# Gate and up projections as seven half-block products in fp32, with the down projection after them

## The chip, the cores and the metric

One core of a Trainium2 chip runs the whole kernel in one launch. The metric is the device time of one execution in microseconds (us).

## What is computed

One layer of a streaming encoder: RMS norm, an input projection, two mixers (a state-space group and a chunk-band attention group), an output projection with a residual, and then the feed-forward part. 1024 new frames and 32 frames of a running stream pass through it, 1056 tokens of width 1024. All data are fp32. The part that matters here is the last two lines of `layer`, with `D_FF` = 2816 = 22 blocks of 128:

```python
x = x + jnp.concatenate([y_ssd, o], axis=-1) @ w_out
f = rmsnorm(x, norm_ffn_g)
x = x + (jax.nn.silu(f @ w_gate) * (f @ w_up)) @ w_down
```

## The kernel before

A product of two fp32 matrices is made of three TensorE products: each operand is split into `hi` (rounded to the type fp32r) and `lo` (what is left of it), and hi·hi, hi·lo and lo·hi are summed in PSUM. `split_unit` (L123 to L131) does this for a 512 KB block of weights: SyncE (SP) issues its load into a `raw` buffer, ScalarE (ACT) casts `whi` (L129), and VectorE (DVE) or GpSimd (POOL) subtracts to get `wlo` (L130). The pool `wp` has 3 buffers of `raw` and 5 each of `whi` and `wlo`, shared by all stages. A tiling framework orders the instructions of every engine ahead of time, by the order of the program and by when it reckons that operands and buffers are there, and inserts the semaphores; on the chip every engine then runs its list in that fixed order.

**The tail of the mixer stage** (L842 to L863). Eight tiles of 128 tokens pass through `wout_tile` (second half of the output projection, residual added at L773) and `norm_transpose`: ACT squares and sums (L189), DVE takes the reciprocal root in a dozen short operations (L138 to L146) and scales (`xn`, L192), PE transposes 8 blocks into PSUM (L197), ACT casts `fT_hi` (L200) and DVE subtracts `fT_lo` (L201). `sample_norm` (L802) puts the 32 tokens of the running stream into columns 1024 to 1055. So `fT` and `fL` hold f transposed, 8 blocks of 128 features by 1056 tokens, in hi and lo.

**The feed-forward stage** (L869 to L947). For each of the 22 blocks f of D_FF, `act_block` computes gate and up: `feat_gemm` (L157 to L162) takes 352 tokens at a time (j = 0, 1, 2), 8 blocks of features and 3 products, so 24 matmuls of 352 columns into one PSUM bank. ACT applies SiLU from PSUM (L897), DVE multiplies from PSUM (L895). Then ACT and DVE split the 1024 columns of `act` into `ahi` and `alo` (L910, L911), which stay in SBUF. After every second block, `down` multiplies them with two blocks of `w_down`: for each of 8 token tiles 12 matmuls of 512 columns (`mm3`, L153 to L155), which DVE adds from PSUM to an accumulator `yacc` (L933) that starts out as the residual, loaded once from DRAM. The sample tokens take 8 short matmuls per pair of blocks (L921). The framework mixes the matmuls of `down` with those of the next blocks' gate and up. For the first block, L903 takes j = 0 of gate and up first, which needs the tokens of tiles 0 to 2 alone.

Of the kernel before, what the change touches and what calls it, by code (L numbers as in the profile page):

```python
# [40 lines left out]
def build(tc, a):  # L41
# [142 lines left out]
    def norm_transpose(pl, x, rows, g, dhi, dlo, c0, raw=None, bufs=2, tb="s"):  # L184
# [13 lines left out]
        tv = t.rearrange("p (q c) -> p q c", q=2)[:, :, 0:4 * rows].rearrange("p q (j c) -> p q j c", j=4)  # L198
        h, l = (d[:, :, c0:c0 + rows].rearrange("p (q j) c -> p q j c", q=2) for d in (dhi, dlo))
        nc.scalar.copy(out=h, in_=tv)  # L200
        nc.vector.tensor_tensor(l, tv, h, op=ALU.subtract)  # L201
        if raw is not None:
            nc.vector.tensor_copy(raw.rearrange("p (q j) c -> p q j c", q=2), tv)
# [14 lines left out]
    def norm_tile(t):  # L218
# [6 lines left out]
        steps = norm_transpose(px, x, rows, gmix, hT, hL, t * P, raw=xsT if t == 8 else None)  # L225
        yield from steps
# [572 lines left out]
    fT = hp.tile([P, KB, NT], F32R, tag="hi", name="fT_hi")  # L799
    fL = hp.tile([P, KB, NT], F32R, tag="lo", name="fT_lo")  # L800

    def sample_norm():  # L802
# [22 lines left out]
        for b in range(2):  # L825
            tv = tb[:, b * P:(b + 1) * P].rearrange("p (g q) -> p g q", g=4)
            h = fT[:, b::2, SB:NT]
            nc.scalar.copy(out=h, in_=tv)
            nc.vector.tensor_tensor(fL[:, b::2, SB:NT], tv, h, op=ALU.subtract)
# [36 lines left out]
    yp = pool("yp")  # L869
# [149 lines left out]
```

## Time and profile before

| | us |
|---|---|
| median of 3 runs (1441.91 to 1445.79) | 1445.55 |
| the profiled execution, its own time | 1441.97 |
| its span, first to last instruction | 1440.3 |
| PE busy in the span | 1377.3 (96%) |
| DVE, ACT, POOL busy in the span | 735.5, 387.1, 204.4 |
| mean granted TensorE clock | 0.986 of 2.4 GHz |

Times in the rows are microseconds unless marked ns; L12 is line 12 of the kernel before. PE is the matmul side of TensorE, PEld its weight loads, which overlap the matmuls; DVE is VectorE, ACT ScalarE, POOL GpSimd, SP SyncE with its DMA queue. Matmuls are pipelined, and the profile models their ends, so the duration of one says little; the distance between two starts says what one costs in a stream.

### The profile page before, as it was taken

What the parts mean: (1) busy time and instruction counts of PE and PEld (TensorE: products, weight loads), DVE (VectorE), ACT (ScalarE), POOL (GpSimd) and SP (SyncE); (2) the same over time, 40 slices, a digit from 0 to 9 for tenths busy, and PEclk for the clock granted to TensorE, in tenths of its full rate; (3) what the DMA queues carried; (4) which work ended last, traced back from release to release, by engine and by line L of the source; (5) the groups of instructions that cost most, each with busy time, mean ns of one, the idle gap of its engine ahead of it and who ended that gap; (6) DMA issues with size and microseconds to landing.
All of it is one profiled execution on the core that took longest, in us unless ns stands there. A gap on an engine that the chain in (4) does not pass through costs nothing.

```text
span 1440.3 us, 21840 instructions
## 1 busy us (share of the span) xinstructions
PE 1377.3 (96%) x8864; PEld 1250.0 (87%) x8864; DVE 735.5 (51%) x1506; ACT 387.1 (27%) x711; POOL 204.4 (14%) x193
## 2 busy tenths in 40 slices
PE   5999999779988999999999999999999999999998
PEld 3999998779976778788999999999989898989897
DVE  7446559999987556675232323242423232323323
ACT  6235331323256444434111111111111111112010
POOL 3142255665322101000000000000000000000000
PEclk8999999989999999999999999999999999999999
DMA  6255242447367985756202020202010101010103
GB/s 239 89 189 160 91 155 71 139 142 233 119 212 226 317 264 173 230 162 245 77 15 73 16 73 15 74 23 66 30 59 30 59 30 59 30 59 30 59 1 121
DMA packets 104900, 160.39 MB, mean 111 GB/s; under 512 B 15680, under 2 KB 74112, under 8 KB 104800
## 3 DMA queue, kind: packets, MB, share of 16 engines
q1 hardware_dynamic: 104800, 159.00, 33.7%
q8 instruction: 70, 1.15, 0.3%
q14 instruction: 30, 0.25, 0.1%
HBM read 108.71 MB, written 50.26 MB: 110 GB/s over the span
## 4 chain that ended last, share of the span: by engine, by line
PE 78%; DVE 13%; DMA 5%; issue 2%; ACT 1%; SPq 1%; POOL 0%; DVEq 0%; ACTq 0%; POOLq 0%
PE ps_mm L160 14%; PE ps_mm L162 14%; PE ps_mm L161 13%; PE ps_s L153 6%; PE ps_s L154 6%; PE ps_s L155 6%; PE ps_mm L153 4%; PE ps_mm L154 3%; PE ps_mm L155 3%; PE ps_mm L728 2%; PE ps_t L711 1%; PE ps_t L921 1%; DVE rs_t L145 1%; PE ps_s L689 1%; DVE e L554 1%
## 5 line engine op out<-in xcount | busy, mean ns | idle before, releaser
L160 PE MATMUL ps_mm<-fT_hi,whi 128*128 128x352 f32 x1056 | 341.9, 324 | 0.9 <-DVE x L773 0.9
L162 PE MATMUL ps_mm<-fT_hi,wlo 128*128 128x352 f32 x1056 | 341.3, 323 | 0.0
L161 PE MATMUL ps_mm<-fT_lo,whi 128*128 128x352 f32 x1056 | 339.5, 321 | 0.1
L933 DVE TENSOR_TENSOR yacc<-ps_s,yacc 128x1024 f32<-128x1024 f32 (+1 forms) x89 | 107.8, 1213 | 205.6 <-PE ps_s L155 205.6
L129 ACT CAST whi<-raw 128x1024 fp32r<-128x1024 f32 (+1 forms) x98 | 101.6, 1049 | 388.4 <-PE ps_mm L161 355.7
L160 PEld LDWEIGHTS ps_mm<-fT_hi,whi 128*128 128x128 f32 x1056 | 198.1, 188 | 7.7 <-issue 4.1
L162 PEld LDWEIGHTS ps_mm<-fT_hi,wlo 128*128 128x128 f32 x1056 | 198.8, 188 | 5.3 <-issue 4.1
L161 PEld LDWEIGHTS ps_mm<-fT_lo,whi 128*128 128x128 f32 x1056 | 198.7, 188 | 3.2 <-DVE fT_lo L201 0.4
L153 PE MATMUL ps_mm<-whi,hT_hi 128*128 128x256 f32 (+1 forms) x512 | 150.8, 295 | 3.7 <-ACT hT_hi L200 3.7
L155 PE MATMUL ps_mm<-whi,hT_lo 128*128 128x256 f32 (+1 forms) x512 | 149.8, 293 | 0.8 <-DVE hT_lo L201 0.8
L154 PE MATMUL ps_mm<-wlo,hT_hi 128*128 128x256 f32 (+1 forms) x512 | 149.5, 292 | 0.0
L153 PE MATMUL ps_s<-whi,ahi 128*128 128x512 f32 x352 | 138.7, 394 | 0.0
L154 PE MATMUL ps_s<-wlo,ahi 128*128 128x512 f32 x352 | 137.5, 391 | 0.0
L155 PE MATMUL ps_s<-whi,alo 128*128 128x512 f32 x352 | 135.5, 390 | 0.0
L130 DVE TENSOR_TENSOR wlo<-raw,whi 128x1024 fp32r<-128x1024 f32 x66 | 79.8, 1223 | 100.9 <-ACT whi L129 100.1
L895 DVE TENSOR_TENSOR act<-ps_mm,act 128x352 f32<-128x352 f32 x66 | 34.6, 525 | 180.3 <-PE ps_mm L162 179.8
L153 PEld LDWEIGHTS ps_mm<-whi,hT_hi 128*128 128x128 f32 x512 | 100.7, 197 | 6.4 <-ACT hT_hi L200 4.4
L155 PEld LDWEIGHTS ps_mm<-whi,hT_lo 128*128 128x128 f32 x512 | 100.7, 197 | 1.5 <-DVE hT_lo L201 1.1
L154 PEld LDWEIGHTS ps_mm<-wlo,hT_hi 128*128 128x128 f32 x512 | 100.5, 196 | 0.7 <-issue 0.4
L130 POOL TENSOR_TENSOR wlo<-raw,whi 128x1024 fp32r<-128x1024 f32 (+1 forms) x32 | 77.7, 2435 | 160.6 <-ACT whi L129 159.3
L897 ACT ACTIVATE act<-ps_mm 128x352 f32<-128x352 f32 x66 | 30.5, 462 | 241.4 <-PE ps_mm L162 241.4
L153 PEld LDWEIGHTS ps_s<-whi,ahi 128*128 128x128 f32 x352 | 66.1, 188 | 16.1 <-PE ps_mm L162 4.1
(226 smaller groups left out, 2140.6 us busy)
## 6 DMA issues: line engine op xcount, KB each, us to landing
raw<-in_wgu_dram SPq DMA_DIRECT2D x44, 512.0 KB, 3.4
raw<-in_wd_dram SPq DMA_DIRECT2D x22, 512.0 KB, 4.0
x<-in_xp_dram SPq DMA_DIRECT2D x16, 512.0 KB, 8.1
q<-qst_d SPq DMA_DIRECT2D x32, 256.0 KB, 4.5
mx<-mix_d SPq DMA_DIRECT2D x16, 512.0 KB, 4.5
raw<-in_wq_dram SPq DMA_DIRECT2D x14, 512.0 KB, 4.3
k<-kst_d SPq DMA_DIRECT2D x8, 528.0 KB, 5.5
raw<-in_wx_dram SPq DMA_DIRECT2D x8, 512.0 KB, 4.8
```

Of the source, the lines that this page charges most:

```text
L129: nc.scalar.copy(out=hi, in_=raw)
L130: (eng or nc.gpsimd).tensor_tensor(lo, raw, hi, op=ALU.subtract)
L153: nc.tensor.matmul(ps_, lhsT=lh, rhs=rh, start=start, stop=False)
L154: nc.tensor.matmul(ps_, lhsT=lh, rhs=rl, start=False, stop=False)
L155: nc.tensor.matmul(ps_, lhsT=ll, rhs=rh, start=False, stop=stop)
L160: nc.tensor.matmul(pb[:, 0:G3], lhsT=wh[:, kb, :], rhs=rh[:, kb, c], start=(kb == 0), stop=False)
L161: nc.tensor.matmul(pb[:, 0:G3], lhsT=wh[:, kb, :], rhs=rl[:, kb, c], start=False, stop=False)
L162: nc.tensor.matmul(pb[:, 0:G3], lhsT=wl[:, kb, :], rhs=rh[:, kb, c], start=False, stop=(kb == KB - 1))
L728: nc.tensor.matmul(ob[64 * h:64 * h + 64, 0:nq], lhsT=vs[j][:nkeys[j], 64 * h:64 * h + 64], rhs=rhs, start=(j == 0), stop=(j == nb - 1), t ...
L895: nc.vector.tensor_tensor(act[:, c], pb[:, 0:G3], act[:, c], op=ALU.mult)
L897: nc.scalar.activation(act[:, c], pb[:, 0:G3], AF.Silu)
L933: nc.vector.tensor_tensor(acc_[:, t, w], pb[:, w], acc_[:, t, w], op=ALU.add)
```

## The change

Gate and up are computed by one level of Strassen's algorithm in Winograd's form. Tokens are cut into halves of 528 (512 of the new frames and 16 of the running stream), the 1024 features into halves of 4 blocks of 128, and D_FF into pairs of blocks of 128. Each pair (gate or up, block pair n) is a `quad`: seven products of a 128x512 weight operand with a 512x528 activation operand, in place of eight. A product is 4 blocks of features, 3 terms (hi·hi, hi·lo, lo·hi) and 2 column halves of 264 tokens, so 24 matmuls of 264 columns, into a two-bank PSUM tile of which there are four. There are 22 quads.

- `norm_transpose` ends in a function `put`. In the tail, `put_half` fills `fA` (hi and lo of the first token half, all 8 feature blocks) and `fR` (all of f in plain fp32; ACT copies it from PSUM). `half_sums` makes the sums of quarters in `fR`, in place, on POOL for tiles 4 to 6 and the sample columns and on DVE for tile 7.
- After the tail, five sums are split on whole quarters of 4x528 columns into `T2`, `B22`, `T1`, `T3`, `T4` (ACT casts, DVE subtracts). `sc`, the scratch of the quads, takes the buffer of `fR` (pool `hp`, tag `lo`, one buffer).
- `prep` loads two weight blocks, forms four sums of 512 columns on POOL in place, and makes four split tiles: X (two quarters), V and U (two sums each), W (one quarter). It is called one quad ahead. It draws on the same 5 buffers of `whi` and `wlo`.
- `quad` makes the products in the order A11·B11, S2·T2, A12·B21, S1·T1, S3·T3, S4·B22, A22·T4; ACT copies the first out of PSUM, DVE adds the others from PSUM, seven additions of 528 columns. SiLU and the product of gate and up now read and write SBUF. The finished activations go to DRAM (`act_d`), 4 DMAs per up quad; POOL copies the sample columns.
- The down projection is a loop of its own after the last quad. `act_unit` loads an activation block from `act_d` and splits it; the accumulator is filled by ACT with the first chunk, and the residual is loaded per tile and added by POOL in the second chunk. Its matmuls are those of before.
- The PSUM pool `ps` is closed after the tail, and `pv` takes all 8 banks.

```diff
-    def norm_transpose(pl, x, rows, g, dhi, dlo, c0, raw=None, bufs=2, tb="s"):
+    def norm_transpose(pl, x, rows, g, put, bufs=2, tb="s"):
...
+    fA = hp.tile([P, 2, KB, H], F32R, tag="hi", name="fA")
+    fR = hp.tile([P, KB, 2, H], F32, tag="lo", name="fR")
+    def put_half(kb, half, c, tv):
+        if half == 0:
...
+            nc.scalar.copy(out=hi, in_=tv)
+            nc.vector.tensor_tensor(lo, tv, hi, op=ALU.subtract)
+        r = fR[:, kb, half, c]
+        nc.scalar.copy(out=quads(r) if kb.step is None else r, in_=tv)
+    def half_sums(c, eng):
+        r11, r21, r12, r22 = (fR[:, 4 * k:4 * k + 4, h, c] for h in range(2) for k in range(2))
+        eng.tensor_tensor(r12, r22, r12, op=ALU.subtract)
+        eng.tensor_tensor(r11, r12, r11, op=ALU.add)
+        eng.tensor_tensor(r21, r21, r11, op=ALU.subtract)
...
+        if t >= 4:
+            half_sums(c, nc.vector if t == 7 else nc.gpsimd)
...
+    split_T(T2, r11)
+    split_T(B22, r22)
+    nc.vector.tensor_tensor(r22, r22, r11, op=ALU.subtract)
+    split_T(T1, r22)
+    split_T(T3, r12)
+    split_T(T4, r21)
...
+    sc = hp.tile([P, KB * NT], F32, tag="lo", name="sc")
...
+    def prep(which, n):
+        r1, r2 = (wp.tile([P, 1024], F32, tag="raw", bufs=3, name=nm("raw")) for _ in range(2))
+        for r, f in ((r1, 2 * n), (r2, 2 * n + 1)):
+            nc.sync.dma_start(r, a["wgu"][f, which])
+        a11, a12, a21, a22 = r1[:, 0:512], r1[:, 512:1024], r2[:, 0:512], r2[:, 512:1024]
+        X, V, U, W = ([wp.tile([P, 1024], F32R, tag=tag, bufs=5, name=nm(tag)) for tag in ("whi", "wlo")]
+                      for _ in range(4))
...
+        split(X, r1)
+        split(W, a22)
+        nc.gpsimd.tensor_tensor(a11, a11, a21, op=ALU.subtract)
+        nc.gpsimd.tensor_tensor(a21, a21, a22, op=ALU.add)
+        nc.gpsimd.tensor_tensor(a22, a22, a11, op=ALU.subtract)
+        split(V, r2)
+        nc.gpsimd.tensor_tensor(a12, a12, a22, op=ALU.subtract)
+        split(U, r1)
...
+    def product(A, B):
+        pb = wide()
+        out = in_psum(pb)
+        terms = [(kb, x, y) for kb in range(4) for x, y in ((0, 0), (0, 1), (1, 0))]
+        for n, (kb, x, y) in enumerate(terms):
+            for h in range(2):
+                nc.tensor.matmul(out[:, h, :], lhsT=A[x][:, kb, :], rhs=B[:, y, kb, h * Q:(h + 1) * Q],
+                                 start=(n == 0), stop=(n == len(terms) - 1))
+        return out
+    def quad(ops, dst, use):
...
+        nc.scalar.copy(out=s1, in_=product(ops["A11"], B11))
+        add(u2, s1, product(ops["S2"], T2))
+        add(d[0][0], s1, product(ops["A12"], B21))
+        use(0, 0)
+        add(v, u2, product(ops["S1"], T1))
+        p7 = product(ops["S3"], T3)
+        add(d[1][1], v, p7)
+        use(1, 1)
+        add(u3, u2, p7)
+        add(d[0][1], v, product(ops["S4"], B22))
+        use(0, 1)
+        add(d[1][0], u3, product(ops["A22"], T4))
+        use(1, 0)
...
+            nc.vector.tensor_tensor(o, o, gates[b][h], op=ALU.mult)
+            nc.sync.dma_start(act_d[2 * n + b, :, h, :], o)
+            nc.gpsimd.tensor_copy(asm[:, 2 * n + b, 16 * h:16 * h + 16], o[:, 512:H])
...
+    work = [(w, n) for n in range(NF // 2) for w in range(2)]
+    ops = prep(*work[0])
+    for k, (w, n) in enumerate(work):
+        cur, ops = ops, prep(*work[k + 1]) if k + 1 < len(work) else None
+        quad(cur, acts if w else gates, use_up(n) if w else use_gate)
...
+    def act_unit(f):
+        raw = p5.tile([P, 2, 512], F32, tag="arow", bufs=2, name=nm("arow"))
+        nc.sync.dma_start(raw, act_d[f, :, :, 0:512])
...
+            if first:
+                nc.scalar.copy(out=acc_[:, t, :], in_=pb)
+                continue
+            if c0 == FC:
+                x = p5.tile([P, 1024], F32, tag="res", bufs=2, name=nm("res"))
+                nc.sync.dma_start(x, xb_d[c])
+                nc.gpsimd.tensor_tensor(acc_[:, t, :], x, acc_[:, t, :], op=ALU.add)
...
+    for c0 in range(0, NF, FC):
+        down(c0)
```

## Rows read from the trace of the kernel before

**Rows 1.** The page: busy time of each engine, and the chain that ended last.

```profile
PE 1377.3 (96%) x8864; PEld 1250.0 (87%) x8864; DVE 735.5 (51%) x1506; ACT 387.1 (27%) x711; POOL 204.4 (14%) x193
...
PE 78%; DVE 13%; DMA 5%; issue 2%; ACT 1%; SPq 1%; POOL 0%; DVEq 0%; ACTq 0%; POOLq 0%
```

**Rows 2.** Busy time by stretch: feed-forward stage; columns as in its first line.

```profile
core 0: us, PE busy (x) PEld busy (x) DVE busy (x) ACT busy (x) POOL busy (x), PEclk, DMA share, GB/s
...
700.00:1400.00 700.00, 700.00 (x3987) 642.21 (x3986) 230.05 (x249) 104.40 (x137) 0.00 (x0) 1.00 0.14 44
```

**Rows 3.** Timeline of PE (start, duration): first and last of 166 consecutive 352-column matmuls.

```profile
745.75 0.32 PE L162 MATMUL ps_mm<-fT_hi,wlo 128*128 128x352 f32 x1
...
772.14 0.32 PE L162 MATMUL ps_mm<-fT_hi,wlo 128*128 128x352 f32 x1
```

**Rows 4.** Timeline of PE: first and last of 48 consecutive 512-column matmuls, last down chunk.

```profile
1424.66 0.39 PE L153 MATMUL ps_s<-whi,ahi 128*128 128x512 f32 x1
...
1435.31 0.39 PE L155 MATMUL ps_s<-whi,alo 128*128 128x512 f32 x1
```

**Rows 5.** The page's costliest groups: gate and up (one of three lines), down (one of three).

```profile
L160 PE MATMUL ps_mm<-fT_hi,whi 128*128 128x352 f32 x1056 | 341.9, 324 | 0.9 <-DVE x L773 0.9
...
L153 PE MATMUL ps_s<-whi,ahi 128*128 128x512 f32 x352 | 138.7, 394 | 0.0
```

**Rows 6.** Timeline of PE: first gate matmul, and the transposes of tile 7.

```profile
661.25 0.43 PE L160 MATMUL ps_mm<-fT_hi,whi 128*128 128x352 f32 x1 [0.89 <-DVE x L773]
...
675.56 1.04 PE L197 MATMUL ps_s<-ident,xn 128*128 128x128 f32 x8
```

**Rows 7.** Timeline of PE: first and last of 15 consecutive 264-column matmuls, input projection.

```profile
59.73 0.28 PE L153 MATMUL ps_mm<-whi,hT_hi 128*128 128x264 f32 x1
...
61.44 0.28 PE L155 MATMUL ps_mm<-whi,hT_lo 128*128 128x264 f32 x1
```

**Rows 8.** Groups by line and shape, DVE, ACT and POOL: busy us, mean ns of one, idle before.

```profile
L933 DVE TENSOR_TENSOR yacc<-ps_s,yacc 128x1024 f32<-128x1024 f32 x87 | 106.5, 1225 | 204.1 <-PE ps_s L155 204.1
L130 DVE TENSOR_TENSOR wlo<-raw,whi 128x1024 fp32r<-128x1024 f32 x66 | 79.8, 1223 | 100.9 <-ACT whi L129 100.1
...
L773 DVE TENSOR_TENSOR x<-ps_mm,x 128x512 f32<-128x512 f32 x32 | 22.0, 691 | 28.2 <-PE ps_mm L155 22.2 <-DMA x<-xa_d 3.1 <-DMA x<-in_xp_dram 2.2
...
L145 DVE SCALAR_TENSOR_TENSOR rs_t<-rs_t,rs_m 128x1 f32<-128x1 f32 x78 | 14.9, 192 | 0.9
...
L129 ACT CAST whi<-raw 128x1024 fp32r<-128x1024 f32 x96 | 99.4, 1049 | 385.6 <-PE ps_mm L161 355.7 <-PE ps_s L155 11.3 <-issue 7.3
...
L189 ACT ACTIVATE sqx<-x 128x1024 bf16<-128x1024 f32 x16 | 16.9, 1059 | 20.5 <-DVE x L773 8.3 <-issue 5.7 <-DVE rs_r L146 4.1
...
L606 ACT CAST yt<-ps_t 128x512 fp32r<-128x512 f32 x8 | 4.7, 584 | 15.3 <-PE ps_t L600 14.3 <-DMA xb<-tok_d 1.0
...
L558 POOL TENSOR_TENSOR xde<-xdt,de 128x512 f32<-128x512 f32 x9 | 9.4, 1040 | 8.4 <-DVE xdt L556 8.4
```

**Rows 9.** Timeline of DVE: a product of two SBUF operands, 512 columns.

```profile
252.37 1.75 DVE L592 TENSOR_TENSOR y<-y,zz 128x512 f32<-128x512 f32 x1
```

**Rows 10.** Timeline of POOL in the same stretch.

```profile
251.86 1.72 POOL L554 TENSOR_TENSOR e<-e,gm 128x512 f32<-128x512 f32 x1
```

**Rows 11.** The page's DMA issues: KB each, median us from issue to landing.

```profile
raw<-in_wgu_dram SPq DMA_DIRECT2D x44, 512.0 KB, 3.4
```

**Rows 12.** Timeline of DVE: tile 7, residual added (two halves), scaled.

```profile
660.50 1.29 DVE L773 TENSOR_TENSOR x<-ps_mm,x 128x512 f32<-128x512 f32 x2 [0.59 <-DMA x<-xa_d]
...
671.15 1.29 DVE L192 SCALAR_TENSOR_TENSOR xn<-x,rs_r,gffn 128x1024 f32<-128x1024 f32 x1 [0.23 <-PE ps_s L197]
```

**Rows 13.** Timeline of PE after an idle time: 256-column matmuls.

```profile
293.46 1.12 PE L600 MATMUL ps_t<-ident,y 128*128 128x128 f32 x4 [3.84 <-DVE gm L550]
...
294.80 0.41 PE L153 MATMUL ps_mm<-whi,hT_hi 128*128 128x256 f32 x1
...
297.36 0.41 PE L153 MATMUL ps_mm<-whi,hT_hi 128*128 128x256 f32 x1
```

More of the change, by code (lines that the diff above doesn't have):

```diff
@@ L22 @@
 G3 = 352
+H = NT // 2
+Q = H // 2
 BIG = 1e30
@@ L197, in norm_transpose, with quads @@
             nc.tensor.transpose(t[:, c:c + rows], xn[:rows, j * P:(j + 1) * P], ident[:rows, :rows])
[L198 to L203, printed above, removed]
+        put(t.rearrange("p (q c) -> p q c", q=2)[:, :, 0:4 * rows].rearrange("p q (j c) -> p q j c", j=4))
+    def quads(v):
+        return v.rearrange("p (q j) c -> p q j c", q=2)
     hT = hp.tile([P, KB, NT], F32R, tag="hi", name="hT_hi")
@@ L224, in norm_tile, with put @@
         yield
-        steps = norm_transpose(px, x, rows, gmix, hT, hL, t * P, raw=xsT if t == 8 else None)
-        yield from steps
+        def put(tv):
+            h, l = (quads(d[:, :, t * P:t * P + rows]) for d in (hT, hL))
+            nc.scalar.copy(out=h, in_=tv)
+            nc.vector.tensor_tensor(l, tv, h, op=ALU.subtract)
+            if t == 8:
+                nc.vector.tensor_copy(quads(xsT), tv)
+        yield from norm_transpose(px, x, rows, gmix, put)
     def z_load(hs):
@@ L826, in sample_norm @@
             tv = tb[:, b * P:(b + 1) * P].rearrange("p (g q) -> p g q", g=4)
[L827 to L829 removed]
+            for half in range(2):
+                put_half(slice(b, KB, 2), half, slice(512, H), tv[:, :, 16 * half:16 * half + 16])
+        half_sums(slice(512, H), nc.gpsimd)
     def first_half():
@@ L915, in down @@
-    def down(chunk, last):
-        nfc = len(chunk)
-        ws = [unit_of("d", f) for f, _ in chunk]
-        pb = bank("t")
-        for k, (f, (_, _, sm)) in enumerate(chunk):
+    def act_unit(f):
+        raw = p5.tile([P, 2, 512], F32, tag="arow", bufs=2, name=nm("arow"))
+        nc.sync.dma_start(raw, act_d[f, :, :, 0:512])
+        hi, lo = (p5.tile([P, SB], F32R, tag=tag, bufs=4, name=nm(tag)) for tag in ("ahi", "alo"))
+        rf = raw.rearrange("p h c -> p (h c)")
+        nc.scalar.copy(out=hi, in_=rf)
+        nc.vector.tensor_tensor(lo, rf, hi, op=ALU.subtract)
+        return hi, lo
@@ L920, in down, with unit_of @@
+    ready = {}
+    def unit_of(f):
+        for g in range(f, min(f + 3, NF)):
+            if g not in ready:
+                ready[g] = act_unit(g), split_unit(a["wd"][g], nc.vector)
+        return ready[f]
+    def down(c0):
+        first, last = c0 == 0, c0 + FC == NF
+        chunk = [unit_of(f) for f in range(c0, c0 + FC)]
+        pb = wide()
+        for k in range(FC):
             for g in range(4):
-                nc.tensor.matmul(pb[32 * g:32 * g + 32, 0:256], lhsT=sm, rhs=ws[k][0][:, g * 256:(g + 1) * 256],
-                                 start=(k == 0), stop=(k == nfc - 1), tile_position=(0, 32 * g))
+                nc.tensor.matmul(pb[32 * g:32 * g + 32, 0:256], lhsT=asm[:, c0 + k, :],
+                                 rhs=chunk[k][1][0][:, g * 256:(g + 1) * 256],
+                                 start=(k == 0), stop=(k == FC - 1), tile_position=(0, 32 * g))
```

103 lines of the change are left out of this document (51 added, 52 removed).

## The prediction

> **What bounds the kernel now.** I read the page first. PE is busy for 96% of the span and stands for 78% of the chain that ended last [rows 1]. Busy shares of matmuls say little, so the next view is the busy time by stretch: from 700 to 1400 us PE never idles, at full clock, while DVE is busy 230 us of 700, ACT 104 and POOL not at all [rows 2]. The stage that the change rewrites is bound by PE's issue of matmuls alone. What a matmul costs there is the distance between starts. 166 matmuls of 352 columns start over 26.39 us, 165 steps of 0.160 us [rows 3]; 48 of 512 columns over 10.65 us, 47 steps of 0.2266 us [rows 4]. Gate and up are 3 x 1056 of the first, down 3 x 352 of the second [rows 5]. From the first gate matmul at 661.25 us [rows 6] to the last start at 1435.31 [rows 4] are 774.1 us: 3168 x 0.160 = 506.6, 1056 x 0.2266 = 239.3, two groups of transposes at 1.04 [rows 6] 2, and 26 left for the sample tokens and the switches between streams.
>
> **The matmuls.** After the change there are 22 quads x 7 products x 24 = 3696 matmuls of 264 columns. The trace has that very shape, in the input projection: 15 of them start over 1.71 us, 14 steps of 0.122 us [rows 7], in hi and lo terms and with a new weight load each, as in the change. 3696 x 0.122 = 451.4 us, so PE saves **55 us**. The columns fall by an eighth (63 us); the rest goes into 528 more switches of weights. One product takes 24 x 0.122 = 2.93 us, one quad 20.5.
>
> One rule speaks against this. The Trainium skill (TensorE: Matmul & The Clock Gate, Back-to-back issue gap) gives the sustained spacing of weight load and matmul pairs as 81 ns at 128 columns and 131 ns at 512; a straight line between them gives 110 ns at 352 and 99 at 264, so 349 us before and 365 after, a loss of 16. The trace does not agree with it: at 512 columns 227 ns stand there against 131 [rows 4].
>
> **Work per quad beside PE.** Lines through the rows: DVE 0.157 us + 1.043 ns a column (1024: 1.225, 512: 0.691), ACT 0.12 us + 0.91 ns (1.049, 0.584), POOL 1.04 us for 512 [rows 8]. DVE: seven additions of 528 columns at 0.71, splits of 3 x 1.22 + 0.69, on average two products at 0.71: 10.7 us. ACT: splits 3.7, one copy 0.6, on average two SiLUs 1.2: 5.5. POOL: 4.2 and two short copies. DVE operations on two SBUF operands stand behind POOL: one of 0.69 us took 1.75, ending 0.54 after the POOL operation that it met [rows 9, 10]. Even with POOL's 4.2 us added whole, DVE has 15 of 20.5. So PE stays the bound, if operands arrive in time. Loads are two of 512 KB in 20.5 us, 3.4 us each [rows 11]; up adds four stores, which SP issues in order, each waiting for DVE's product; a load behind one has some 10 us to spare. POOL's short copies wait for DVE's product too, and the next weight sum is queued behind them; that wait is in the chain's delays below. I take 0 for the rest.
>
> **The operand chain, each quad.** Four split tiles a quad share five buffers, so the next quad's X is split early and the last of its other three waits for a buffer that product 6 of this quad holds. If that one is W (the order of allocation), the second product of the next quad hangs on: W cast 0.58, subtract 0.69, POOL 1.04, V cast 1.05, subtract 1.22 = 4.6 us. It is covered by product 7 and the next product 1, 5.9 us: 1.3 to spare. DVE can have an addition and a product ahead (1.4), and a POOL operation can hold it up (1.04): 2.4 of delay, 1.1 beyond cover. If buffers are given in order of need, nothing waits. I take 0.3 us, nearer to the covered end since the delays need not meet: 21 x 0.3 = **+6**, ends 0 and 34 (1.6 each, should a cast wait on ACT as well).
>
> **The start.** Today j = 0 of the first block fills PE while tiles 6 and 7 finish: tile 7's transposes start 14.3 us after the first gate matmul [rows 6]. After, only products 1 and 3 need `fA` alone; the others need sums over all tiles. Tile 7's residual is done at 661.8; its scaling ends at 672.4 [rows 12] behind four weight splits. Undisturbed it would be square 1.06, a dozen short operations of 0.19, scaling 1.29 [rows 8, 12]: 666.5. I take 669.5, between. Then transposes 1.0 [rows 6], ACT's copy 1.0: 671.5. DVE now has three sums of 512 (2.1) and six operations on 2112 columns at 2.36 (14.2): 687.7, and with two POOL operations in the way 689.8. Only then is `fR` free, so that ACT can copy product 1 out (0.6). All four PSUM tiles are full by then, with four products made; the other three take 8.8: 699.2. PE has idled for spells of several us; after 3.84 us of idle time the trace shows 12 steps of 0.213 us at 256 columns, the 1.2 GHz level [rows 13]. I add 1.5 for that: 700.7. Without the wait the first quad and two groups of transposes would end at 661.25 + 22.5 = 683.8. The start costs **+17**. Ends: 9 (scaling at 666.5, no POOL, no slow clock) and 28 (scaling at 675, DVE busy with 4.3 of weight splits in between, slow clock for all three products).
>
> **Down alone.** The same 1056 matmuls and 88 short ones. DVE has per chunk eight additions of 1.225 and four splits of 1.22, 14.7 of about 23 us. In the second chunk POOL adds eight residuals, about 2.1 each, below the 2.7 that PE needs per tile. Today 26 us go into switches and sample tokens scattered between streams; here they come in one group a chunk: **-4**, ends 0 and -10. The handover from the last quad: loads of activations may start while its last products run, since their space is the first T tiles'; **+2**, ends 0 and 10 (a load 4, cast and subtract 2.3 for each of two blocks). The tail has one ACT copy of 1.0 more for tiles 0 to 3 and POOL sums of 3.1 for tiles 4 to 6; ACT has idle time there and POOL nothing else: 0, ends -1 and 3.
>
> **Sum.** -55 + 6 + 17 - 4 + 2 = -34. The profiled execution took 1441.97, its span 1440.3, so I predict **1408**. That execution stands at the low end of the three runs, whose median is 3.6 higher; I add nothing for that.
>
> **Rivals.**
> 1. *The operand chain paces the quads*, though less than the gain: both delays meet each time, 0.8 to 1.6 us a quad, 17 to 34 in place of 6, so 1419 to 1436. For it: POOL and DVE hinder each other [rows 9, 10]. Against: 1.3 us to spare, and the order of PE may take product 3, which needs X alone, ahead of 2.
> 2. *The handovers are long*: both at their upper ends, 28 + 10 in place of 19, 1427. For it: the scratch takes the buffer of `fR`, so nothing evacuates early. Against: products 1 and 3 have no need of it.
> 3. *Slower.* The buffer for which the chain waits is that of product 7, not 6. Then only the next product 1 covers it: 4.6 + 1.4 - 2.9 = 3.1 us a quad, 65 in all, in place of 6: 1467. It decides from 2.3 us a quad on: 21 x 2.3 = 48 takes the 40 of gain that is left without this term, and 8 more bring it 0.3% above the median. For it: five buffers for four live tiles. Against: W is the only tile read by product 7 and the other three are free before.
> 4. *The count of matmuls is what is paid for*, not their columns: 3696 x 0.160 = 591, 85 more, 1441.97 + 85 + 21 = 1548. Against it: 264 columns at 0.122 [rows 7]; only another layout of the operands could bring it. The Trainium skill's rule named above would also give a loss, a smaller one; this chance includes it.
>
> **Chances.** Forecast 0.61, rival 1 0.16, rival 2 0.08, rival 3 0.12, rival 4 0.03. A difference of 0.3% (4.3 us) is about what can be told from none. The forecast, rival 2 and nearly all of rival 1 are faster; the upper edge of 1 and the lower of 3 reach into no difference: faster 0.82, same 0.05, slower 0.13. The range takes in the forecast with its ends and rivals 1 and 2: 1392 to 1438. Its low end is -55 + 0 + 11 - 7 + 1 = -50, since the lower ends need not all meet; above 1438 are rivals 3 and 4.
>
> **What would show it.** Right: 264-column matmuls 0.122 apart; quads repeating every 20.5 to 21 us, with PE idle at most 0.3 on average; one idle stretch of some 15 us in pieces between 662 and 700, waiting for DVE's splits; down at 0.2266. Wrong: an idle time of PE before the second product of every quad, ended by DVE or ACT of the weight split (rivals 1, 3); PE idle for over 5 us before the first down matmul (2); a spacing near 0.16 (4).

## The result and the profile after

| | before | after |
|---|---|---|
| median, us | 1445.7 (1441.9 to 1446.9) | 1413.3 (1409.8 to 1413.9) |
| the profiled execution, its span | 1441.97, 1440.3 | 1412.81, 1411.0 |
| mean granted clock of TensorE | 0.986 | 0.973 |

The ratio of the times is 0.9775, with a 95% interval from 0.9751 to 0.9799: 32 us faster where 38 were forecast from the median and 34 from the profiled execution.

The page of the changed kernel, busy time of the engines and the chain that ended last, which answers to [rows 1]:

```profile
PE 1321.3 (94%) x9392; PEld 1203.3 (85%) x9392; DVE 894.8 (63%) x1657; ACT 459.9 (33%) x776; POOL 385.8 (27%) x345
...
PE 74%; DVE 16%; DMA 6%; issue 2%; ACT 2%; SPq 1%; DVEq 0%; POOL 0%; ACTq 0%
```

Busy time by stretch of the same kernel, columns as in its first line. It answers to [rows 2]: from 720 us on PE is full at full clock as before, with DVE at half. Between 660 and 720 us it is not, and the granted clock falls.

```profile
core 0: us, PE busy (x) PEld busy (x) DVE busy (x) ACT busy (x) POOL busy (x), PEclk, DMA share, GB/s
...
660.00:680.00 20.00, 8.54 (x40) 6.50 (x39) 16.16 (x32) 7.56 (x10) 11.98 (x10) 0.78 0.32 104
680.00:700.00 20.00, 11.53 (x58) 11.14 (x58) 16.65 (x13) 9.07 (x7) 4.39 (x3) 0.62 0.09 29
700.00:720.00 20.00, 18.02 (x135) 18.02 (x136) 13.53 (x14) 9.38 (x11) 4.57 (x2) 0.91 0.15 50
720.00:1140.00 420.00, 420.00 (x3435) 420.00 (x3435) 212.34 (x265) 113.38 (x142) 132.43 (x121) 1.00 0.22 77
```

Timeline of ACT (start, duration): the copy of the first product out of PSUM, which opens each quad, here of quads 1 and 21.

```profile
721.17 0.60 ACT L981 COPY sc<-ps_w 128x528 f32<-128x528 f32 x1 [1.61 <-PE ps_w L972]
...
1132.30 0.60 ACT L981 COPY sc<-ps_w 128x528 f32<-128x528 f32 x1 [1.61 <-PE ps_w L972]
```

Twenty quads in 411.13 us, 20.56 each, 0.1224 for each of 168 matmuls. PE waits for nothing in between, so the operand chain costs nothing.

Timeline of PE: the first matmul of down, and the start of the last.

```profile
1154.23 0.50 PE L157 MATMUL ps_w<-whi,ahi 128*128 128x512 f32 x1 [3.40 <-ACT ahi L1028]
...
1406.16 0.39 PE L159 MATMUL ps_w<-whi,alo 128*128 128x512 f32 x1
```

So down takes 251.9 us, and 1.1 for the sample matmuls that stand ahead of the wait of 3.40. Against 239.3 + 26 before that is 12 less.

| term | forecast, us | measured, us |
|---|---|---|
| matmuls of gate and up | -55 | 3696 x 0.1224 - 506.6 = -54 |
| operand chain | +6 (0 to 34) | 0 |
| start | +17 (9 to 28) | first quad ends at 717.98, against 683.8: +34 |
| down alone | -4 (-10 to 0) | -12 |
| handover | +2 (0 to 10) | +3 |
| sum | -34 | -29, the change of the span |

The sum is near because errors of both signs meet in it: +17 and two of +1 against -6 and -8. That is luck. The start is the largest error, and lies outside its own bounds. Here it is on PE's timeline:

```profile
685.97 1.94 PE L201 MATMUL ps_s<-ident,xn 128*128 128x128 f32 x8 [10.22 <-DVE xn L196]
687.57 1.23 PE L972 MATMUL ps_w<-fA,whi 128*128 128x264 f32 x4
...
694.71 0.53 PE L972 MATMUL ps_w<-T,whi 128*128 128x264 f32 x2 [2.16 <-ACT T L919]
...
701.98 1.25 PE L972 MATMUL ps_w<-T,whi 128*128 128x264 f32 x4 [2.32 <-ACT T L919]
```

The reader sees two things. Tile 7's transposes, at 675.56 before [rows 6], wait until 685.97 for its scaling (`xn`). Then PE waits twice more, for casts of T tiles. DVE's timeline shows what tile 7 went through (`x` is the residual, the 128x1 operations its reciprocal root, `wlo` splits of weights):

```profile
671.30 0.68 DVE L783 TENSOR_TENSOR x<-ps_mm,x 128x512 f32<-128x512 f32 x1
...
673.59 0.14 DVE L142 TENSOR_SCALAR rs_m<-ss 128x1 f32<-128x1 f32 x1
...
674.85 1.19 DVE L149 SCALAR_TENSOR_TENSOR rs_t<-rs_t,rs_m 128x1 f32<-128x1 f32 x1
675.96 1.21 DVE L949 TENSOR_TENSOR wlo<-raw,whi 128x1024 fp32r<-128x1024 f32 x1
677.10 1.22 DVE L150 SCALAR_TENSOR_TENSOR rs_r<-rs_t,rs_r 128x1 f32<-128x1 f32 x1
678.36 0.16 DVE L148 TENSOR_TENSOR rs_t<-rs_r 128x1 f32<-128x1 f32 x1
678.55 1.12 DVE L149 SCALAR_TENSOR_TENSOR rs_t<-rs_t,rs_m 128x1 f32<-128x1 f32 x1
...
683.54 2.29 DVE L196 SCALAR_TENSOR_TENSOR xn<-x,rs_r,gffn 128x1024 f32<-128x1024 f32 x1
```

And POOL's in the same microseconds:

```profile
672.55 2.25 POOL L958 TENSOR_TENSOR raw<-raw,raw 128x512 f32<-128x512 f32 x1
674.76 1.27 POOL L829 TENSOR_TENSOR fR<-fR 128x512 f32<-128x512 f32 x1
676.88 1.43 POOL L827 TENSOR_TENSOR fR<-fR 128x512 f32<-128x512 f32 x1 [0.86 <-ACT fR L822]
678.38 1.27 POOL L828 TENSOR_TENSOR fR<-fR 128x512 f32<-128x512 f32 x1
```

An operation on one number per partition takes 0.16 us alone and 1.1 to 1.2 beside a POOL sum. The Trainium skill (SBUF — State Buffer, SBUF: two separate sides) says that a DVE operation with two SBUF inputs and a GpSimd operation that reads SBUF need the same port pair: the one that starts first has it for the whole instruction, and the other waits. The trace agrees: the long `rs_t` and `rs_r`, with two inputs, end within 0.02 us of POOL's operation, and `rs_m` with one (0.14) is not held by the POOL operation of 672.55.

### The profile page after: what moved, and what is told of

It reads as the page before. It is cut to its first block, busy times and chain, and to the rows that moved or that the text cites. A ratio compares the mean times of both kernels' runs of the same rounds, so it can differ in the third digit from the quotient of the medians.

```text
span 1411.0 us, 23744 instructions
## 1 busy us (share of the span) xinstructions
PE 1321.3 (94%) x9392; PEld 1203.3 (85%) x9392; DVE 894.8 (63%) x1657; ACT 459.9 (33%) x776; POOL 385.8 (27%) x345
## 4 chain that ended last, share of the span: by engine, by line
PE 74%; DVE 16%; DMA 6%; issue 2%; ACT 2%; SPq 1%; DVEq 0%; POOL 0%; ACTq 0%
PE ps_w L972 32%; PE ps_w L157 6%; PE ps_w L158 6%; PE ps_w L159 6%; PE ps_mm L157 4%; PE ps_mm L158 3%; PE ps_mm L159 3%; PE ps_mm L738 2%; PE ps_mm L164 2%; PE ps_mm L166 2%; PE ps_mm L165 2%; PE ps_t L721 2%; DVE rs_t L148 2%; DMA qst_d<-st 2%; DVE rs_r L150 2%
## 5 line engine op out<-in xcount | busy, mean ns | idle before, releaser
L980 DVE TENSOR_TENSOR sc<-sc,ps_w 128x528 f32<-128x528 f32 x154 | 106.4, 703 | 205.4 <-PE ps_w L972 205.4
L972 PE MATMUL ps_w<-T,whi 128*128 128x264 f32 x1408 | 231.0, 286 | 4.5 <-ACT T L919 4.5
L972 PEld LDWEIGHTS ps_w<-T,whi 128*128 128x128 f32 x1408 | 196.7, 189 | 4.9 <-ACT T L919 4.9
L972 PE MATMUL ps_w<-T,wlo 128*128 128x264 f32 x704 | 144.0, 286 | 0.0
L157 PE MATMUL ps_w<-whi,ahi 128*128 128x512 f32 x352 | 138.4, 393 | 3.4 <-ACT ahi L1028 3.4
L158 PE MATMUL ps_w<-wlo,ahi 128*128 128x512 f32 x352 | 137.3, 390 | 0.0
L159 PE MATMUL ps_w<-whi,alo 128*128 128x512 f32 x352 | 136.0, 389 | 0.0
L972 PE MATMUL ps_w<-fA,whi 128*128 128x264 f32 x704 | 117.4, 290 | 0.0
L972 PEld LDWEIGHTS ps_w<-T,wlo 128*128 128x128 f32 x704 | 109.6, 189 | 0.0
L949 DVE TENSOR_TENSOR wlo<-raw,whi 128x1024 fp32r<-128x1024 f32 x88 | 98.2, 1116 | 11.6 <-ACT whi L948 10.2
L972 PEld LDWEIGHTS ps_w<-fA,whi 128*128 128x128 f32 x704 | 100.3, 193 | 0.0
```

Of the source, the lines that this page charges most:

```text
L157: nc.tensor.matmul(ps_, lhsT=lh, rhs=rh, start=start, stop=False)
L158: nc.tensor.matmul(ps_, lhsT=lh, rhs=rl, start=False, stop=False)
L159: nc.tensor.matmul(ps_, lhsT=ll, rhs=rh, start=False, stop=stop)
L949: nc.vector.tensor_tensor(t[1][:, 0:w], src, t[0][:, 0:w], op=ALU.subtract)
L972: nc.tensor.matmul(out[:, h, :], lhsT=A[x][:, kb, :], rhs=B[:, y, kb, h * Q:(h + 1) * Q], start=(n == 0), stop=(n == len(terms) - 1))
L980: add = lambda o, x, y: nc.vector.tensor_tensor(o, x, y, op=ALU.add)
```

## The experiments

My theory A after this reading: what was gained is columns of PE, and what was lost is tile 7's lateness, caused by POOL's sums. In the table, the residual and the scaling of tile 7 (when each ends) and the first copy of quad 1 mark the start in each trace. Medians carry some 3 us of uncertainty: by intervals that do not meet, only runs 9 and 12 stand apart from the changed kernel as faster. The marks come from one trace each, and carry what came before the tail: run 9, which changes nothing ahead of quad 0, scales tile 7 2.1 us earlier than the changed kernel, and run 5, whose tail is that of the kernel before, 2.6 later than that. Counted from the start of tile 1's transposes (column "tile 1 to scaled") this goes away: 58.5, 58.6 and 58.5 for the changed kernel and runs 7 and 9, 51.6 and 52.0 for the kernel before and run 5. That column says what a cause is worth. The transposes of tile 1, in the kernel before and the changed one:

```profile
620.80 1.09 PE L197 MATMUL ps_s<-ident,xn 128*128 128x128 f32 x8
...
627.34 1.09 PE L201 MATMUL ps_s<-ident,xn 128*128 128x128 f32 x8
```

| kernel | residual | scaled | tile 1 to scaled | copy, quad 1 | median, us |
|---|---|---|---|---|---|
| before | 661.8 | 672.4 | 51.6 | | 1445.7 |
| after | 672.0 | 685.8 | 58.5 | 721.2 | 1413.3 |
| 1 sums of quarters on DVE | 666.6 | 680.2 | 55.6 | 714.6 | 1410.3 |
| 2 weight sums on DVE | 673.3 | 685.8 | 57.4 | 721.2 | 1409.6 |
| 3 both on DVE | 666.4 | 679.4 | 53.9 | 713.8 | 1407.5 |
| 4 down alone, four PSUM tiles | 663.6 | 674.3 | 51.4 | | 1456.9 |
| 5 down alone, old PSUM tiles | 664.5 | 675.0 | 52.0 | | 1441.1 |
| 6 quad 0 without weight work | 669.6 | 679.7 | 57.4 | 713.4 | 1408.8 |
| 7 scratch in quarters of `fR` | 672.0 | 685.8 | 58.6 | 721.2 | 1411.1 |
| 8 early products | 667.1 | 681.9 | 56.9 | 716.8 | 1411.0 |
| 9 another order in quad 0 | 669.9 | 683.7 | 58.5 | 713.1 | 1406.6 |
| 10 all in one | 667.8 | 682.6 | 56.9 | 719.2 | 1410.4 |
| 11 four weight buffers | 671.9 | 682.0 | 57.5 | 718.4 | 1412.6 (one run) |
| 12 order and DVE sums | 665.1 | 678.2 | 53.9 | 709.7 | 1401.5 |

**1 to 3. POOL's sums go to DVE.**

```diff
-            half_sums(c, nc.vector if t == 7 else nc.gpsimd)
+            half_sums(c, nc.vector)
...
+        eng = nc.vector if n == 0 else nc.gpsimd
-        nc.gpsimd.tensor_tensor(a11, a11, a21, op=ALU.subtract)
+        eng.tensor_tensor(a11, a11, a21, op=ALU.subtract)
```

The first pair of lines (and one like it for the sample columns) is run 1, the others (and three like them) are run 2.

> All sums of quarters (tiles 4 to 6, sample columns) move from POOL to DVE; nothing else. Theory A (the first quad ends late because tile 7's scaling is late, 685.8 us in place of the 669.5 forecast, and it is late because DVE's short operations on SBUF stand behind POOL's sums, 1.1 to 1.25 us each in place of 0.16): tile 7's scaling ends 4 to 8 us earlier although DVE gets 9 sums of 0.69 us more, the first quad ends near 713, the kernel takes 1405 to 1410. Rival B (what is late is fixed by the order of PE's list and by the clock, not by POOL): within 1.5 us of the changed kernel, 1413. Rival C (DVE itself is full in the tail, whoever shares its port): 3 to 6 us slower than the changed kernel.

> The weight sums of the first two quads (8 operations on 512 columns) move from POOL to DVE. Theory A: the DVE operation that took 2.24 us at 586 loses its partner, so that the first transposes of the tail are 3 to 6 us earlier, and of the four that met tile 7's reciprocal root two go; 1406 to 1411. Rival B: no difference (1412 to 1415), since the loss at 586 to 600 is a fall of the clock that comes anyway. Rival C: 2 to 5 us slower.

> Both moves: POOL does nothing between 590 and 720 us but splits of the output projection's weights. Theory A: no DVE operation in the tail lasts longer than alone (short ones 0.16 us), tile 7's scaling ends at 672 to 678, the first quad at 702 to 708, the kernel takes 1398 to 1406. Rival B: 1412 to 1415. Rival C: 1416 to 1422, with DVE busy without a gap from 664 to 705.

In run 1 the scaling comes 5.6 us earlier, as theory A said, with a ratio to the kernel before of 0.9759 (0.9737 to 0.9781). But 2.7 of the 5.6 stand already at tile 1's transposes, ahead of the sums of tiles 4 to 6; 2.9 can be theirs. Run 2 missed its forecast: tile 0's transposes came 4.0 us earlier (612.4 against 616.4), but tile 1's 1.1 later (628.5 against 627.3), and the scaling did not move. I had misread the tail's beginning: the DVE operation of 2.24 us at 586 stood beside a weight split of the output projection on POOL, and the sums came only at 591. Its ratio, 0.9762 (0.9731 to 0.9793), cannot be told from the change's own, 0.9775 (0.9751 to 0.9799), and neither can that of run 1. Run 3 has no POOL sum near tile 7 and no long short operation, yet its scaling ends at 679.4, not at 672 to 678, and its 1407.5 lies above the range of theory A. DVE's timeline of run 3 shows why:

```profile
673.68 0.15 DVE L148 TENSOR_TENSOR rs_t<-rs_r 128x1 f32<-128x1 f32 x1
673.80 0.69 DVE L955 TENSOR_TENSOR raw<-raw,raw 128x512 f32<-128x512 f32 x1
674.41 0.15 DVE L149 SCALAR_TENSOR_TENSOR rs_t<-rs_t,rs_m 128x1 f32<-128x1 f32 x1
674.48 0.68 DVE L827 TENSOR_TENSOR fR<-fR 128x512 f32<-128x512 f32 x1
675.08 0.68 DVE L956 TENSOR_TENSOR raw<-raw 128x512 f32<-128x512 f32 x1
675.68 0.15 DVE L150 SCALAR_TENSOR_TENSOR rs_r<-rs_t,rs_r 128x1 f32<-128x1 f32 x1
```

DVE's own list has sums and weight work between tile 7's short operations. From residual to scaling it is 13.0 us, against 13.9 with POOL and 10.6 in the kernel before. What run 3 wins lies mostly ahead of the residual: from tile 1's transposes to it are 40.9 us, 41.0 in the kernel before and 44.6 in the changed one. So of the 6.9 us that the change adds between tile 1's transposes and tile 7's scaling, 4.6 go when the sums leave POOL, and 2.3 stay, as work that the change put into DVE's list. How much of the 4.6 is the port alone is not shown, since runs 2, 3, 8, 10 and 12 also have another order in the lists (tile 0's transposes start 16.1 us ahead of tile 1's, 11.0 in the changed kernel and in run 1).

**4 and 5. Down alone.** Both keep gate and up as they were (3168 matmuls of 352 columns, no sums of quarters), send activations through DRAM and run the changed kernel's loop of down. Run 4 also takes the changed kernel's PSUM pool of four two-bank tiles, opened after the tail:

```diff
-        pb = bank("mm")
+        pb = wide()
         feat_gemm(pb, wh, wl, fT, fL, j)
...
-        nc.scalar.copy(out=hi, in_=act[:, 0:SB])
+        nc.sync.dma_start(act_d[f], act)
```

> No Strassen: gate and up as in the kernel before, 3168 matmuls of 352 columns, but activations pass through DRAM and down is a stage of its own, with the changed kernel's loops. Theory A (the stage of down alone gives back some 13 us of switches between streams and costs 3.4 at its start, whatever makes gate and up): 1445.6 - 13 + 3 = 1436, between 1432 and 1439; the columns then account for 1413 - 1436 = -23 net of the start's +34, so -57. Rival (the short distance of down in the changed kernel comes from Strassen's products, not from the separation): 1445 to 1449, the handover alone.

It missed on the other side: 1.0086 (1.0058 to 1.0113) of the kernel before. PE's timeline tells where: 

```profile
674.47 1.94 PE L201 MATMUL ps_s<-ident,xn 128*128 128x128 f32 x8 [4.03 <-DVE xn L196]
678.77 0.66 PE L164 MATMUL ps_w<-fT_hi,whi 128*128 128x352 f32 x1 [2.36 <-DVE fT_lo L859]
...
1196.01 0.79 PE L157 MATMUL ps_w<-whi,ahi 128*128 128x512 f32 x1 [10.23 <-ACT ahi L936]
...
1450.55 0.39 PE L159 MATMUL ps_w<-whi,alo 128*128 128x512 f32 x1
```

Gate and up start behind tile 7's transposes, 17.5 us later than in the kernel before [rows 6], and down waits 10.2 for loads whose space came free only at the end. The stage of down itself takes 254.5 us, of which some 2.5 are a first tile at the low clock. So the saving is there, and its surroundings cost more. Run 4 is also the control for the columns: from the first to the last start, gate and up take 505.7 us in it and 462.0 in the changed kernel, which has 9.7 of waits and low clock in its first quad. Run 5 takes both of these costs away. It keeps the tail's PSUM pool (one-bank tiles for gate and up, two two-bank tiles for down) and has space for the loads from the start.

> The kernel before with down as a stage of its own and nothing else: gate and up keep their PSUM tiles and their place in the lists (so that the first block's j = 0 can run ahead of tile 7 again), activations pass through DRAM, and the space for activation loads is there before gate and up end. In the run with down alone, gate and up started at 678.8 us in place of 661.3, and down waited 11.3 us; inside the stages 503.9 us for gate and up and 252.4 for down at full clock stood against 774 for both together in the kernel before. Theory A (the separation gives back 13 to 16 us of switches, and that run lost them to its own start and handover): 1431 to 1438. Rival (a separate down gives back nothing in total, the gaps only move): 1443 to 1449.

1441.1, ratio 0.9974 (0.9959 to 0.9989): between the two theories, with a quarter of the saving. Its down is slower than that of the changed kernel. The sample matmuls come once in each chunk of down and so show its period. First the changed kernel, then run 5, each with the first and last start of a group of 16:

```profile
L1046 PE MATMUL ps_w<-raw,sc x16: 379/379/403, 1222.3 to 1223.0; 128*32 128x256 f32 x16
L1046 PE MATMUL ps_w<-raw,sc x16: 379/379/403, 1245.3 to 1246.0; 128*32 128x256 f32 x16
```

```profile
L927 PE MATMUL ps_t<-raw,asm x16: 379/391/403, 1280.9 to 1284.7; 128*32 128x256 f32 x16
L927 PE MATMUL ps_t<-raw,asm x16: 379/391/403, 1305.0 to 1308.8; 128*32 128x256 f32 x16
```

23.0 us against 24.1, 11 times over: 11 to 12 us. Without the 96 matmuls at 0.2266 run 5 has 2.35 us left in a chunk, 26 in eleven, as many as the kernel before had with its streams mixed. From the first gate matmul to the last start of down it takes 770.8 us, the kernel before 774.1: the separation alone saves some 3. In run 5 the sample matmuls are cut in two groups, and in each chunk PE waits once for DVE to empty one of the two tiles:

```profile
1253.91 0.50 PE L154 MATMUL ps_s<-whi,ahi 128*128 128x512 f32 x1 [0.42 <-DVE yacc L946]
```

With four tiles (run 4 and the changed kernel: 23.0 both) neither happens. So the 12 us booked under down as a stage of its own point to its four tiles, which the tail's pool, shared with gate and up, does not have. This is argued and not shown: runs 4 and 5 differ in their pools and lists too, and no run changes the number of tiles alone.

**6. Quad 0 without its weight work.**

```diff
         split(X, r1)
+        if (which, n) == (0, 0):
+            x = [[y[:, c:c + 512].rearrange("p (k c) -> p k c", k=4) for y in X] for c in (0, 512)]
+            return dict(A11=x[0], A12=x[1], S1=x[0], S2=x[1], S3=x[0], S4=x[1], A22=x[0])
```

> Leaves work out: quad 0 uses its first weight tile X for all seven products, so its three other splits and its four weight sums fall away (the gate of the first pair of blocks is not the reference's). POOL's sums of quarters stay. Theory D (beside POOL's port it is the weight splits of quad 0 that stand ahead of tile 7's reciprocal root in DVE's list, 4.3 us of them, and POOL's weight sums): tile 7's scaling ends 6 to 9 us earlier than 685.8, the kernel takes 1404 to 1408. Theory A alone (POOL's sums of quarters are the cause): 3 to 4 us earlier at most, 1409 to 1411. Rival B (lists and clock): 1412 to 1415.

Scaling at 679.7, 6.2 us earlier, and 1408.8, ratio 0.9743 (0.9710 to 0.9776): by these, the edge of theory D's ranges. But 5.1 of the 6.2 stand already at tile 1's transposes (622.2 against 627.3), and from there on 1.1 are left. Nor does the place stay empty: the framework moves quad 1's weight work into it, two splits on DVE from 664.9 and four sums on POOL until 676.2. The first and the last of these sums:

```profile
666.20 2.25 POOL L957 TENSOR_TENSOR raw<-raw,raw 128x512 f32<-128x512 f32 x1 [2.59 <-DVE wlo L949]
...
674.98 1.26 POOL L961 TENSOR_TENSOR raw<-raw,raw 128x512 f32<-128x512 f32 x1
```

So this run takes no weight work away from tile 7 and decides between no theories. Run 4 does: without sums of quarters and without the quads' weight work it takes 51.4 us from tile 1's transposes to the scaling, as the kernel before does.

**7. The scratch in quarters of `fR`.**

```diff
-    sc = hp.tile([P, KB * NT], F32, tag="lo", name="sc")
-    piece = [sc[:, n * H:(n + 1) * H] for n in range(14)]
+    piece = [fR[:, kb, 0, :] for kb in range(4)] + [fR[:, kb, 1, :] for kb in range(4, 8)]
+    piece += [fR[:, kb, 1, :] for kb in range(4)] + [fR[:, kb, 0, :] for kb in range(4, 8)]
```

> The scratch of the quads lies in quarters of fR itself instead of a new tile in its place, so that the first product's copy waits for the quarter r11 alone (T2's split and the difference read it last), not for all splits. Theory A (the first quad waits for fR as one buffer): ACT's first copy from PSUM at 697 to 699 in place of 705.4; then the seven products after 687.6 at the low clock of their beginning set the end, 711 to 714 in place of 718, and the kernel takes 1407 to 1410. Rival E (the last split, T4 at 705.4, sets the end whatever the copy does, or PE's clock does): 1412 to 1414.

The first copy came at 701.8 in place of 705.4, and nothing followed: quad 1 opens at 721.2 as before, and the ratio is 0.9758 (0.9730 to 0.9787). So `fR` as one buffer, on which my prediction built the second half of the start, does not set its end. ACT's timeline of the changed kernel shows what does:

```profile
688.99 1.95 ACT L919 CAST B<-fR 128x2112 fp32r<-128x2112 f32 x1
690.85 5.66 ACT L919 CAST T<-fR 128x2112 fp32r<-128x2112 f32 x3
699.46 0.62 ACT L948 CAST whi<-raw 128x512 fp32r<-128x512 f32 x1 [2.95 <-PE ps_w L972]
699.98 1.95 ACT L919 CAST T<-fR 128x2112 fp32r<-128x2112 f32 x1
705.38 0.60 ACT L981 COPY sc<-ps_w 128x528 f32<-128x528 f32 x1 [3.45 <-DVE T L920]
```

`T1` is cast last, until 701.93. Its source is the difference that DVE has ready at 697.9, but in ACT's list the cast stands behind one of a weight tile, which waits until 699.46 for PE to release a buffer. PE's list asks for product 4, the reader of `T1`, before 5 and 6, whose operands are long there. At 701.98 it starts on the last four products (the row above), and 16.0 us later the quad is done.

**8. Products 1 and 3 ahead of tile 7.** They need the first token half alone. This run has both sums on DVE, the scratch of run 7, and puts these two into one-bank tiles of the tail's pool:

```diff
+    ops = prep(*work[0])
+    early = [product(ops[o], B, [bank(tag)[:, 0:Q] for _ in range(2)])
+             for o, B, tag in (("A11", B11, "t"), ("A12", B21, "mm"))]
     tails_end()
```

> Three things together: sums of quarters and the first two quads' weight sums on DVE, the scratch in quarters of fR, and products 1 and 3 of quad 0 (which need the first token half alone) put into PSUM banks of the tail's own pool ahead of tile 7's transposes. Theory A with DVE's chain as the bound: end of quad 0 at T4's split (near 699) plus product 7, 702 to 706 against 718, so 1397 to 1403. Rival B (PE's list and its cold start are the bound): with two products out of the way and PE busy earlier, 697 to 701 and 1392 to 1397. Rival F (the moved parts hinder each other in the lists): 1403 or more.

It was rival F: 1411.0, ratio 0.9752 (0.9732 to 0.9772). Both products run in gaps of the tail, and the copy of quad 1 comes 3.0 us later than in run 3, which lacks them. The scaling comes 2.5 us later, 3.0 counted from tile 1's transposes, for a reason not found (run 10 moves less weight work ahead and has it no earlier), and PE, with nothing else to do, waits for the T tiles at the low clock (granted 0.50 between 680 and 700):

```profile
690.81 0.81 PE L930 MATMUL ps_w<-T,whi 128*128 128x264 f32 x2 [6.79 <-ACT T L964]
696.37 0.81 PE L930 MATMUL ps_w<-T,whi 128*128 128x264 f32 x2 [4.75 <-DVE T L965]
```

**9. Another order of products in quad 0.** The scratch of run 7, and PE asked for products in the order in which their operands come:

```diff
+        made = {}
+        if first:
+            for key, B in (("A11", B11), ("A12", B21), ("S4", B22), ("S3", T3), ("S2", T2), ("S1", T1), ("A22", T4)):
+                made[key] = product(ops[key], B)
```

> As the run with the scratch in quarters of fR (which changed nothing), and in quad 0 alone the products are asked for in the order 1, 3, 6, 5, 2, 4, 7. Theory G (what the first quad waits for is neither DVE's last split nor fR's buffer but ACT's cast of T1, the last of its five, at 701.9 us, since PE's list asks for product 4 before 5 and 6 whose operands are ready; from that cast to the end are four products, 16.0 us): PE works without a wait from the first product at 687.6 on, seven products of 2.93 and some 5 us of low clock, so the quad ends at 712 to 714 in place of 718, and the kernel takes 1406 to 1410. Rival H (the last split or the banks of PSUM bound it anyway, the wait only moves): 716 to 718, 1411 to 1414.

Theory G: 1406.6, ratio 0.9721 (0.9699 to 0.9744). PE works without a wait until 701.8 and idles once:

```profile
703.89 0.39 PE L975 MATMUL ps_w<-T,whi 128*128 128x264 f32 x1 [1.94 <-DVE fR L991]
```

The quad ends at 709.85, 26.2 us after the scaling in place of 32.2. (The scaling came 2.1 earlier here; that stands already at tile 0's transposes, 614.2 against 616.4, ahead of all that the edit touches.) The forecast of 712 to 714 was too careful: the first products left the low clock after some 4 us, and the granted clock stayed at 1.00 from then on, through the one wait too.

**10. All in one**: runs 3, 8 (with the rest of quad 0's weight work left where it was) and 9.

> All that helped in one: sums of quarters and the first weight sums on DVE, scratch in quarters of fR, products 1 and 3 of quad 0 in banks of the tail's pool ahead of tile 7's transposes (the rest of quad 0's weight work stays where it was), then products 6, 5, 2, 4, 7. Theory G: tile 7's scaling ends near 680 as in the run with both sums on DVE, product 6 starts some 10 us later at B22's split, five products and the low clock take 19 to 20 us: the quad ends at 706 to 711 against 718 and 710.9 of that run; the kernel takes 1401 to 1407. Rival H: 712 or later, 1407 to 1412, no better than the sums on DVE alone.

Rival H: 1410.4, ratio 0.9753 (0.9735 to 0.9772). Products 1 and 3 hold four of the eight banks until ACT has copied the one and DVE has added the other, which stands in its list behind the last splits, and PE waits for that:

```profile
702.45 1.25 PE L931 MATMUL ps_w<-T,whi 128*128 128x264 f32 x4 [7.01 <-DVE fR L993]
```

Work that is done early keeps its PSUM for as long as its reader is late.

**11. Four weight buffers.** `bufs=(3, 4, 4)` in `split_unit`, and 4 in `prep`.

> Four buffers of the split weight tiles instead of five, everywhere. Theory A (buffers come free in the order of need, so even the next quad's X and W, after products 3 and 4, and V, after 6, are ready in time): quads repeat every 20.5 to 21 us as in the changed kernel (20.56), the total within 10 us of it. Rival (the chain of V's sums and split is as tight as the prediction's third rival had it, 3.1 us a quad when it waits for product 7): 23 to 24 us a quad, 1460 or more.

1412.6 in one run, and ACT's timeline gives the period:

```profile
718.36 0.60 ACT L981 COPY sc<-ps_w 128x528 f32<-128x528 f32 x1 [1.58 <-PE ps_w L972]
...
1129.49 0.60 ACT L981 COPY sc<-ps_w 128x528 f32<-128x528 f32 x1 [1.58 <-PE ps_w L972]
```

Twenty quads in 411.13 us, 20.56 each. Even one buffer fewer costs the quads nothing; my third rival is refuted with room to spare.

**12. Order and DVE sums**, runs 9 and 3 together, without early products.

> The order 1, 3, 6, 5, 2, 4, 7 in quad 0 with the scratch in quarters of fR, and all sums of the tail and of the first two quads on DVE. If the two causes are separate, they add: tile 7's scaling ends near 679.4 as with both sums on DVE, and from there to the end of quad 0 it takes the 26.2 us of the run with the new order (32.2 in the changed kernel), 705 to 707; the kernel takes 1400 to 1404. If they overlap (the time won by one is a wait for the other's engine), it is no faster than the order alone, 1405 to 1408.

They add by the time: 1401.5 (1399.4 to 1403.6), ratio 0.9689 (0.9668 to 0.9710), the best of all and 12 us below the changed kernel. (From scaling to the end of the quad, at 706.5, it is 28.3 us and not run 9's 26.2: PE waits 2.5 before product 4, and the clock falls.) Scaling ends at 678.2, and the copy of quad 1 comes 11.5 us earlier:

```profile
709.65 0.60 ACT L993 COPY fR<-ps_w 128x528 f32<-128x528 f32 x1 [0.84 <-PE ps_w L976]
```

## Why the prediction was right, and where it was wrong

**What bounds the kernel, and the matmuls: right.** PE's issue stays the bound, and the spacing of 264-column matmuls read from another stage of the kernel before [rows 7], 0.122 us, is 0.1224 in the new one. That is -54 against -55, the larger part of the 66 gained; the rest is down's. The fourth rival would have brought 1548. The Trainium skill's rule named beside it would have brought, by the estimate there, a loss of 16.

**The operand chain: 0 in place of 6.** "If buffers are given in order of need, nothing waits" was the right branch; I had put 0.3 us a quad on the other. Run 11 shows how far off the edge is: with four buffers there is still no wait. Rivals 1 and 3 fall with it. Rival 2 came true in its first half, the start passing its 28; the time does not show it, because down and the operand chain came in below their terms.

**The start: 34 in place of 17, the step that failed.** It is the term "I take 669.5, between" for tile 7's scaling; it ended at 685.8. Of these 16.3, 2.9 are the estimate's own: it lay that much below the kernel before (672.4), as if less stood in DVE's list, and kept that kernel's residual, 661.8, as given. (Of the four weight splits that it names there, one ends ahead of the residual.) Another 6.9 are what the change adds between tile 1's transposes and the scaling: 4.6 go when the sums leave POOL (run 3), and 2.3 are its sums and weight work in DVE's list, between tile 7's short operations. Run 4, without either, has none of the 6.9. The last 6.5 stand already at tile 1's transposes; 2.3 of them are there at 566 us, when the last half tile of the first half of the output projection is added, and no run takes them apart. I had charged POOL 2 us for two operations after the scaling and booked its sums for tiles 4 to 6 at 0 ("ACT has idle time there and POOL nothing else"), though [rows 9, 10] showed what they do to DVE.

The second half, from scaling to the end of the quad, was forecast at 31.2 us and took 32.2, but not by the path described. I had the copy wait for `fR`, then three products. In truth it waits for `T1`, then four products. Run 7 refutes the first, run 9 shows the second: the same T tiles, asked for in another order, take 26.2. A sum that comes out is no evidence for its path.

**Down alone: -12 in place of -4**, below its lower end of -10. I looked for the saving in switches between streams. Runs 4 and 5 point elsewhere: to four PSUM tiles in place of two, about 1.05 us a chunk, though no run changes them alone. That PSUM was divided anew stood in front of me as a change, and I priced it nowhere; in run 4, where gate and up no longer run ahead of tile 7, they start 17.5 us later.

**Handover: 3.4 in place of 2**, near in size, but not by the path described. I had the loads start while the last products run, with only casts to wait for. SP's list has them behind the last quad's stores, which wait for DVE's products; the first load is issued at 1148.8, 0.7 us before the last start of gate and up, so PE waits for the landing and the cast:

```profile
1148.81 1.24 SPq L1025 DMA_DIRECT2D arow<-act_d  x2
...
1153.13 1.04 ACT L1028 CAST ahi<-arow 128x1024 fp32r<-128x1024 f32 x1 [11.23 <-DMA arow<-act_d]
```

What stays open: the residual of tile 7 is 4.6 us later in run 3 than in the kernel before, and all of it is there at tile 1's transposes. Their start spreads from 622.2 to 628.5 us in the kernels with the changed tail and from 620.8 to 623.0 in the kernel before and runs 4 and 5, and no run takes that apart. Down takes from 251.9 to 254.8 us in kernels that have it alike. In runs 1, 3, 8, 10 and 11 its first tile comes at the low clock, which costs some 2.5, and run 7 has 2.2 of waits for PSUM; the rest has no reason found. It limits what the medians of runs 1, 2, 7 and 8 can say.

## What to carry to other kernels

Price an algorithm with fewer products by the spacing that the trace has for the new shape, and then look at its first unit of work: there all the new operands are made at once, on engines whose lists still hold the previous stage. An engine that works off a fixed list waits for the operand that comes last if the list asks for it early, so ask for operands in the order in which they are made; here that and the engine of some sums are worth 12 us. When a change divides PSUM anew, price the number of tiles in every stage, also in those whose arithmetic stays the same. And compare single traces from a mark that the edit cannot have moved: here 6.5 of the 13.4 us by which tile 7 was later stood already at the mark.

## What the runs showed of the hardware

A DVE operation on a single column, 0.16 us alone, takes up to 1.25 us beside a POOL operation if it has two operands in SBUF, and 0.14 if it has one. A dozen of them in a row, as in a reciprocal root, meet POOL again and again: between 659 and 681 us eight took more than 0.3 us in the changed kernel, none in run 3.

After an idle time of 10.2 us the first 264-column matmuls came 0.22 us apart at a granted clock of 0.50 (687.5 to 691.5 us), the 1.2 GHz level, for some 4 us, and then 0.12 apart. After one more wait of 2.2 us shortly behind (694.71 above) they fell back to it (granted 0.55 up to 698.5), and after one of 2.3 once more (0.53 from 702.0 to 705.5). Not every such wait did this: in run 9 one of 1.9 us, behind 12 us of full clock without a pause, left the clock at 1.00, while in run 12 one of 2.5 brought it down. Ahead of down, a wait of 3.4 in the changed kernel left it at 1.00, and one of 3.3 in run 1 was followed by 0.50.
